# First layer: the gate's weights in one 48-column operand, norm vectors loaded by rows, the first head's projections ahead of the small tokens

## The chip, the core and the metric

The kernel runs on one core of a Trainium2 chip. The core has five engines that take their instructions in written order, each from its own queue: TensorE (PE, matrix products; its weight loads are listed apart as PEld), VectorE (DVE), ScalarE (ACT), GpSimd (POOL) and SyncE (SP), which here does nothing but issue DMA transfers. The metric is the device time of one execution in microseconds (us), as the median of several runs.

## The reference

One inference step of a two-layer decoder, in float32. There are 1024 prompt tokens, 16 "meta" tokens in front of them, and 8 sample tokens that continue running sequences, each of 1024 features. Layer one is gated linear attention (4 heads, keys of 128, values of 256), layer two differential attention with a paged cache; a squared-ReLU MLP of 4096 follows each. Cut to what matters here:

```python
def gla_project(x, w_in, w_gate, b_gate):
    h = x @ w_in
    q, k, v, r, g_low = jnp.split(h, [qk, 2 * qk, 2 * qk + vv, 2 * qk + 2 * vv], axis=-1)
    ...
    lg = jax.nn.log_sigmoid((g_low @ w_gate + b_gate).astype(F32)) / GLA_TAU

def gla_chunk(state, q, k, v, lg):
    b = jnp.cumsum(lg, axis=1)
    o_inter = jnp.einsum('blhd,bhde->blhe', q * jnp.exp(b), state)
    ...

def post_norm(x, f, g, b):
    return layer_norm(DEEPNORM_ALPHA * x + f, g, b)
```

`g_low` has 16 columns: the gate is a product with 16 columns of `w_in`, then one with the 16-row matrix `w_gate`.

## The kernel before

**Prompt tokens.** The 1024 prompt tokens are transposed by TensorE (L264) into XH and XL, the high and the low part of x, features on partitions, in two halves of 512 tokens (`c`). A product in near-float32 precision is three matmuls (`mm3`, L194 to L197): high by high, high by low, low by high. Weights come through `unit` (L171): four loads of 256 KB into `raw` (two buffers), a cast on ACT to `whi`, a subtraction on POOL to `wlo`. Two such units exist at a time. `qk_unit(h)` holds head h's q and k columns, `kunit(wi, 1024 + 256h)` its v columns.

**The gate.** `graw` holds the 16 gate columns; `ghi` and `glo` are its parts. For each half, eight blocks of features with three matmuls each go to a bank of PSUM, and a DVE copy brings 16 rows to `gT`: the first half of the tokens on partitions 0 to 15, the second on 32 to 47. `wg` holds `w_gate` twice, on the same partitions.

**Small tokens.** The 16 meta and 8 sample tokens stand together in `sx` (32 columns). They run through all of layer one, its MLP and the input projection of layer two in plain float32, with the small token block as the stationary operand in four column strips of 32 and the weights streaming through `swt` (two buffers of 1 MB). L280 and L285 are their input projection (eight and four loads of 1 MB), L413 their product with the eight running states, three buffers of which lie in Y (`stt`, loaded at L410, updated at L416). L449, L503 and L520 are the later matrices. `SM`, the state behind the meta tokens, is what the prompt's heads start from.

**Heads.** For each of four heads: q and k for both halves (96 matmuls of 512), v (192 matmuls of 256), then for each half the gate product L602, `log_gate` on ACT and DVE, a cumulative sum (L607), the products within 32-token blocks and at seven levels (L617, L632; elementwise work in `level`), and four steps that carry the state (L660 to L664). Products go to three banks named `mmt`, the rest of a head to three banks named `axt`, the small tokens to two named `smt`. Then the r projections with the output gate (L683 to L695), and the stage's pools close.

**Vectors.** `lnp` holds the four pairs of norm vectors with features on partitions: eight loads (L304), each gathering 1024 separate 4-byte elements. `bg` (L309, 512 elements) and `gn` (L564, 256) come in the same way.

**What sets the order.** The program is written in the order of the listing, but a planner orders each engine's instructions before the run: it walks a simulated time line and gives a free engine the ready instruction that was written first. The small tokens are written ahead of the heads, so the heads' projections fill the places where the small tokens wait. The hardware then keeps to that order, whatever really comes late. `tc.issue_after(ins)` places what is traced inside it behind `ins` on its queue.

Of the kernel before, what the change touches and what calls it, by code (L numbers as in the profile page):

```python
# [21 lines left out]
P = 128  # L22
D = 1024
T = 1024
NB = 8
# [3 lines left out]
GH = 4  # L29
# [81 lines left out]
def hybrid_step(ctx, tc, A, dbg=None, upto=9):  # L111
    nc = tc.nc
    V, S, G, TE = nc.vector, nc.scalar, nc.gpsimd, nc.tensor
    dma = nc.sync.dma_start
# [20 lines left out]
    def mmt():  # L135
        return banks["mm"].tile([P, 512], F32, name="mmt")

    def axt():
        return banks["ax"].tile([P, 512], F32, name="axt")

    def smt():
        return banks["sm"].tile([P, 512], F32, name="smt")

    def cload(name, pool=cp):
        a, b = CCOL[name]
        t = pool.tile([P, b - a], F32, name="c_" + name)
        dma(t, A["cf"][:, a:b])
        return t
# [8 lines left out]
    ident = cload("ident")  # L157
# [29 lines left out]
    def kunit(w, c0):  # L187
        return unit(256, w.rearrange("(k p) n -> p k n", p=P)[:, :, c0 : c0 + 256])

    def split(hi, lo, src, eng=V):  # L190
        S.copy(hi, src)
        return eng.tensor_tensor(lo, src, hi.bitcast(F32), op=ALU.subtract)  # L192

    def mm3(ps, ah, al, bh, bl, first, last):  # L194
        TE.matmul(ps, ah, bh, start=first, stop=False)  # L195
        TE.matmul(ps, ah, bl, start=False, stop=False)  # L196
        TE.matmul(ps, al, bh, start=False, stop=last)  # L197
# [3 lines left out]
    gp = p1.enter_context(tc.tile_pool(name="gp", bufs=1))  # L201
    g2 = p1.enter_context(tc.tile_pool(name="g2", bufs=2))
# [23 lines left out]
    def sload2(w, k, eng=None):  # L226

        t = swt()
        dma(t, w[k * P : (k + 2) * P, :].rearrange("(k p) n -> p k n", p=P))
        return t  # L230

    sx = gp.tile([P, NB, TS], F32, name="sx")
    masks = gp.tile([P, 5, TS], U8, name="masks")
    Ats = [gp.tile([P, 4, P], F32, name="At%d" % i) for i in range(2)]
# [12 lines left out]
    ps = smt()  # L247
# [3 lines left out]
    wi = A["gla_w_in"][0]  # L251
    wir = wi.rearrange("(k p) n -> p k n", p=P)

    def qk_unit(h):
        return unit(P, *[wir[:, :, 512 * i + h * P : 512 * i + (h + 1) * P] for i in range(2)])

    qku = qk_unit(0)
    for t in range(4, 8):
        dma(Yt[:, t, :], A["x_prompt"][0, t * P : (t + 1) * P, :])
    for c in range(2):  # L260
        for k in range(NB):
            ps = axt()
            for i in range(4):
                TE.transpose(ps[:, i * P : (i + 1) * P], Yt[:, 4 * c + i, k * P : (k + 1) * P], ident)  # L264
            cs = slice(512 * c, 512 * c + 512)
            split(XH[:, k, cs], XL[:, k, cs], ps)
# [1 line left out]
    mf = s4()[:, : 5 * TS]  # L268
    dma(mf, A["cm"].rearrange("p l t -> p (l t)"))
    V.tensor_copy(masks.rearrange("p l t -> p (l t)"), mf)  # L270
    graw = gp.tile([P, NB, 16], F32, name="graw")
    dma(graw, wir[:, :, 3072:3088])
    diag = cload("diag", gp)


    pa, pb = smt(), smt()
# [4 lines left out]
    for k in range(0, NB, 2):  # L281
        w = sload2(wi[:, 2048:3072], k)
        for i in range(2):
            for c in range(GH):
                TE.matmul(pb[c * TS : (c + 1) * TS, :256], sx[:, k + i, :], w[:, i, c * 256 : (c + 1) * 256], start=k + i == 0, stop=k + i == NB - 1)  # L285
    sqkv = s2()
    S.copy(sqkv, pa)
    sv = Y[:TS, 4096:5120]
# [9 lines left out]

    inv = cload("inv", gp)
    srope = cload("srope", gp)  # L300
    for i, nm in enumerate(("ln_mix", "ln_mlp")):
        for j, gb in enumerate("gb"):
            for l in range(2):
                dma(lnp[:, 2 * l + i, j, :], A[f"{nm}_{gb}"][l].rearrange("(k p) -> p k", p=P))  # L304
    wg = gp.tile([48, 512], F32, name="wg")
    for c in range(2):
        dma(wg[32 * c : 32 * c + 16, :], A["gla_w_gate"][0])
    bg = gp.tile([P, GH], F32, name="bg")
    dma(bg, A["gla_b_gate"][0].rearrange("(h p) -> p h", p=P))  # L309

    def log_gate(z, n, h):

        a = t2()[:, :n]
        S.activation(a, z, AF.Abs, bias=bg[:, h : h + 1])
        S.activation(a, a, AF.Exp, scale=-1.0)
        S.activation(a, a, AF.Ln, bias=1.0)
        m = t2()[:, :n]
        V.tensor_scalar(m, z, bg[:, h : h + 1], 0.0, ALU.add, ALU.min)
        V.tensor_tensor(m, m, a, op=ALU.subtract)
        return m  # L320

    ps = smt()
# [4 lines left out]
    ps = smt()  # L327
# [79 lines left out]
    for b in range(NS):  # L407
        stt = Y[:, 5120 + 1024 * (b % 3) : 6144 + 1024 * (b % 3)].rearrange("p (h e) -> p h e", e=256)
        vb = vbs[:, b % 2, :].rearrange("p (h e) -> p h e", e=256)
        dma(stt, A["state_gla"][0, b].rearrange("h d e -> d h e"))  # L410
        dma(vb.rearrange("p h e -> p (h e)"), A["vs"][b : b + 1, :].broadcast_to([P, D]))
        for h in range(GH):
            TE.matmul(po[h * TS : (h + 1) * TS, :256], qmk[:, h, b, :], stt[:, h, :], start=False, stop=b == NS - 1)  # L413
# [135 lines left out]
    dma(A["sxd"], sx)  # L549


    ghi = gp.tile([P, NB, 16], F32R, name="ghi")
    glo = gp.tile([P, NB, 16], F32R, name="glo")
# [9 lines left out]
    gn = gp.tile([P, 2], F32, name="gn")  # L563
    dma(gn, A["gla_norm"][0].rearrange("(m p) -> p m", p=P))  # L564
    gss = gp.tile([P, GH, 8], F32, name="gss")

    for h in range(GH):
        hi, lo = qku if h == 0 else qk_unit(h)
        hv, lv = (w.rearrange("p (i k n) -> p i k n", i=2, n=P) for w in (hi, lo))
        qk = {}  # L570
        for c in range(2):
            cs = slice(512 * c, 512 * c + 512)
            for i in range(2):
                ps = mmt()
                for k in range(NB):
                    mm3(ps, hv[:, i, k, :], lv[:, i, k, :], XH[:, k, cs], XL[:, k, cs], k == 0, k == NB - 1)
                t = g2.tile([P, 512], F32, name=("gq", "gk")[i])
                if i == 0:
                    S.activation(t, ps, AF.Copy, scale=P ** -0.5)
                else:  # L580
                    S.copy(t, ps)
                qk[c, i] = t
        hi, lo = kunit(wi, 1024 + h * 256)
        hv, lv = (w.rearrange("p (k n) -> p k n", n=256) for w in (hi, lo))
        vt = {}
        for c in range(2):
            v = Yh[:, h, 4 * c : 4 * c + 4, :]
            for i2 in range(2):
                ps = mmt()
                for i in range(2):  # L590
                    t = 4 * c + 2 * i2 + i
                    for k in range(NB):
                        a = slice(t * P, (t + 1) * P)
                        mm3(ps[:, i * 256 : (i + 1) * 256], XH[:, k, a], XL[:, k, a], hv[:, k, :], lv[:, k, :], k == 0, k == NB - 1)
                S.copy(v[:, 2 * i2 : 2 * i2 + 2, :].rearrange("p i e -> p (i e)"), ps)
            vt[c] = v
        st = SM[:, h, :]
        for c in range(2):
            q, k_, v = qk[c, 0], qk[c, 1], vt[c]
            cs = slice(512 * c, 512 * c + 512)  # L600
            ps = axt()
            TE.matmul(ps, wg[32 * c : 32 * c + 16, h * P : (h + 1) * P], gT[32 * c : 32 * c + 16, :], start=True, stop=True)  # L602
# [945 lines left out]
```

## Time and profile before

| | |
|---|---|
| median of 3 runs | 2934.85 us (2927.28, 2934.85, 2936.18) |
| profiled execution, its own time | 2915.81 us |
| its span, first to last instruction | 2914.1 us |
| mean granted TensorE clock | 0.978 |
| PE / PEld / DVE / ACT / POOL busy, share of the span | 96 / 78 / 64 / 36 / 39% |
| last output of the small tokens' chain issued | 410 us |
| first load of layer two issued | 506 us |

A line of the order of time reads: start in us, duration in us, engine, line of the kernel, operation, what is written and what is read, shape, number of instructions; in brackets, the idle time before it and who ended it. A line of waits reads: who waited, for whom, total us, times, longest. "SPq" is SyncE's queue of DMA issues. In a row by stretches, each engine has its busy time and its number of instructions in brackets; then come the granted clock (1.00 is full speed), the share of time in which the DMA engines were busy, and the rate. Durations of matmuls are modelled and overlap: the spacing of their starts is what they take.

### The profile page before, as it was taken

The page shows a single profiled execution, that of the slowest core. Times are in us where ns is not written, and L with a number is a line of the kernel's source. Part 1 is how long each engine was busy: PE and PEld are TensorE (multiplying, and loading weights), DVE is VectorE, ACT ScalarE, POOL GpSimd, SP SyncE. Part 2 cuts the span into 40 slices and gives each one's busy share as a digit, 9 for nine tenths or more (in the row PEclk, how much of TensorE's full clock was granted, in tenths as well). Part 3 has the DMA queues.
Part 4 walks back from the last instruction along what each step waited for, and adds up shares of the span by engine and source line. Part 5 has one row for each costly group of instructions (what it writes and reads, how often), then busy time and mean ns, then how long its engine had stood idle before and what let it go on. Part 6 is the DMA issues. An engine that isn't in the chain of part 4 may idle for free. (4 is left out here: it accounts for less than half of the span.)

```text
span 2914.1 us, 52192 instructions
## 1 busy us (share of the span) xinstructions
PE 2783.9 (96%) x19668; PEld 2275.1 (78%) x19668; DVE 1857.9 (64%) x2976; ACT 1038.3 (36%) x2071; POOL 1145.4 (39%) x885
## 2 busy tenths in 40 slices
PE   8999999999999999999989999989898999999996
PEld 5776668987777777777888986878788889797985
DVE  2664544458877877777676731878438755838378
ACT  2343354151122122122411111777325535345343
POOL 1321122234333333433323430122326766677666
PEclk9999999999999999999999998999899999999998
DMA  8667541524798888988488988463427878796972
GB/s 262 210 214 248 187 168 39 191 73 164 255 341 309 309 328 310 331 315 321 137 274 288 360 298 260 102 135 84 116 98 214 230 224 234 195 288 163 270 205 86
DMA packets 299308, 643.83 MB, mean 221 GB/s; under 512 B 35168, under 2 KB 150880, under 8 KB 287792
## 3 DMA queue, kind: packets, MB, share of 16 engines
q1 hardware_dynamic: 267520, 531.15, 52.8%
q0 software_dynamic: 31536, 109.35, 15.2%
q8 instruction: 155, 2.54, 0.3%
q14 instruction: 97, 0.79, 0.1%
HBM read 582.89 MB, written 40.91 MB: 214 GB/s over the span
## 5 line engine op out<-in xcount | busy, mean ns | idle before, releaser
L183 POOL TENSOR_TENSOR wlo<-raw,whi 128x512 fp32r<-128x512 f32 x256 | 361.2, 1425 | 786.0 <-ACT whi L182 697.6
L195 PE MATMUL mmt<-whi,XH 128*128 128x256 f32 (+1 forms) x1824 | 554.0, 305 | 7.5 <-DVE qr L1051 3.8
L196 PE MATMUL mmt<-wlo,XH 128*128 128x256 f32 (+1 forms) x1824 | 550.8, 303 | 0.5 <-POOL wlo L183 0.5
L195 PE MATMUL mmt<-XH,whi 128*128 128x512 f32 (+1 forms) x1376 | 480.1, 350 | 15.7 <-DVE HL L192 6.4
L197 PE MATMUL mmt<-XH,wlo 128*128 128x512 f32 (+1 forms) x1376 | 479.4, 350 | 0.0
L197 PE MATMUL mmt<-whi,XL 128*128 128x256 f32 x1536 | 440.5, 287 | 6.8 <-DVE XL L192 6.8
L195 PEld LDWEIGHTS mmt<-whi,XH 128*128 128x128 f32 x1824 | 346.3, 190 | 43.6 <-issue 19.8
L182 ACT CAST whi<-raw 128x512 fp32r<-128x512 f32 x256 | 152.4, 619 | 619.0 <-PE mmt L197 247.3
L196 PEld LDWEIGHTS mmt<-wlo,XH 128*128 128x128 f32 x1824 | 346.6, 190 | 25.0 <-issue 11.7
L771 DVE TENSOR_REDUCE sc<-pg 128x16 f32<-128x1024 f32 x256 | 309.6, 1214 | 78.4 <-POOL pg L770 74.9
L197 PEld LDWEIGHTS mmt<-whi,XL 128*128 128x128 f32 x1536 | 292.3, 190 | 22.7 <-issue 14.8
L196 PE MATMUL mmt<-XL,whi 128*128 128x512 f32 x768 | 307.6, 400 | 0.0
L195 PEld LDWEIGHTS mmt<-XH,whi 128*128 128x128 f32 x1376 | 261.2, 190 | 57.5 <-DVE HL L192 8.2
L770 DVE TENSOR_TENSOR pg<-pg,qb 128x1024 f32<-128x1024 f32 x192 | 261.3, 1366 | 59.1 <-DMA pg<-in_cache_k 42.9
L197 PEld LDWEIGHTS mmt<-XH,wlo 128*128 128x128 f32 x1376 | 261.2, 190 | 43.6 <-issue 12.0
L770 POOL TENSOR_TENSOR pg<-pg,qb 128x1024 f32<-128x1024 f32 x64 | 156.3, 2443 | 286.3 <-DMA pg<-in_cache_k 215.0
L195 PE MATMUL mmt<-whi,HH 128*128 128x512 f32 x512 | 205.3, 401 | 1.4 <-DVE Y L995 1.4
L196 PE MATMUL mmt<-wlo,HH 128*128 128x512 f32 x512 | 204.5, 399 | 0.0
L197 PE MATMUL mmt<-whi,HL 128*128 128x512 f32 x512 | 203.7, 398 | 0.0
L196 PEld LDWEIGHTS mmt<-XL,whi 128*128 128x128 f32 x768 | 145.2, 189 | 40.4 <-issue 8.9
L196 PE MATMUL mmt<-XH,whi 128*128 128x258 f32 x608 | 173.0, 286 | 3.7 <-DMA XH<-xc 2.9
L1397 POOL TENSOR_TENSOR wlo<-RW,whi 128x512 fp32r<-128x512 f32 x96 | 152.4, 1678 | 56.6 <-ACT whi L1396 56.5
(432 smaller groups left out, 5482.1 us busy)
## 6 DMA issues: line engine op xcount, KB each, us to landing
pg<-in_cache_k SPq DMA_DIRECT2D x256, 512.0 KB
pg<-in_cache_v SPq DMA_DIRECT2D x256, 512.0 KB
XH<-xc POOLq DMA_DIRECT2D x42, 1032.0 KB, 8.8
raw<-in_mlp_w SPq DMA_DIRECT2D x164, 256.0 KB
rw<-in_mlp_w SPq DMA_DIRECT2D x156, 256.0 KB
swt<-in_mlp_w SPq DMA_DIRECT2D x32, 1024.0 KB
RW<-in_mlp_w POOLq DMA_DIRECT2D x96, 256.0 KB, 7.3
xc<-XH POOLq DMA_DIRECT2D x14, 1032.0 KB, 8.0
```

Source lines behind the costliest of these rows:

```text
L182: S.copy(hi[:, c], raw)
L183: G.tensor_tensor(lo[:, c], raw, hi[:, c].bitcast(F32), op=ALU.subtract)
L195: TE.matmul(ps, ah, bh, start=first, stop=False)
L196: TE.matmul(ps, ah, bl, start=False, stop=False)
L197: TE.matmul(ps, al, bh, start=False, stop=last)
L770: eng.tensor_tensor(pg, pg, qb, op=ALU.mult)
L771: return V.tensor_reduce(sc[:, n, :], pg.rearrange("p (h d) -> p h d", d=64), op=ALU.add, axis=AX.X).ins
L1397: G.tensor_tensor(lo[:, k, :], t, hi[:, k, :].bitcast(F32), op=ALU.subtract)
```

## The change

The stage of layer one is changed in these ways; nothing of layer two is.

1. The gate's high and low parts stand in one 48-column operand `gw` (high in columns 0 to 15, zeros, low in 32 to 47). Each block of features is multiplied with XH and with XL, 2 matmuls in place of 3, and two groups of 16 rows of the result are added. The product of low part and low part is thereby included.
2. The norm vectors, the gate's bias and the output norm are loaded by six transfers of rows of 128 elements into one tile, turned by one transpose, and spread by four copies.
3. `proj(h)` holds a head's q, k and v projections. The gate and `proj(0)` are written ahead of the small tokens' input projection; the first head's v weights are loaded ahead of the transposes.
4. The states' loads are placed behind the last load of the small tokens' input weights on SyncE's queue.
5. For each head both halves' gate products are written one behind the other, each with a bank of its own, ahead of the work of the halves.

```diff
@@ sload2
-        dma(t, w[k * P : (k + 2) * P, :].rearrange("(k p) n -> p k n", p=P))
+        swl.append(dma(t, w[k * P : (k + 2) * P, :].rearrange("(k p) n -> p k n", p=P)).ins)
...
@@ before the transposes of x
+    v0u = kunit(wi, 1024)
+    graw = gp.tile([P, NB, 16], F32, name="graw")
+    dma(graw, wir[:, :, 3072:3088])
...
@@ behind the load of the masks
-    graw = gp.tile([P, NB, 16], F32, name="graw")
-    dma(graw, wir[:, :, 3072:3088])
     diag = cload("diag", gp)
+
+    prow = s2()[:, :P]
+    for i, nm in enumerate(("ln_mix", "ln_mlp")):
+        for j, gb in enumerate("gb"):
+            dma(prow[32 * i + 16 * j : 32 * i + 16 * j + 16, :], A[f"{nm}_{gb}"].rearrange("l (k p) -> (l k) p", p=P))
+    dma(prow[64:68, :], A["gla_b_gate"].rearrange("l (h p) -> (l h) p", p=P))
+    dma(prow[68:70, :], A["gla_norm"].rearrange("l (m p) -> (l m) p", p=P))
+    ps = smt()
+    TE.transpose(ps[:, :70], prow[:70, :], ident[:70, :70])
+    for i in range(2):
+        V.tensor_copy(lnp[:, i::2].rearrange("p l j k -> p j l k"), ps[:, 32 * i : 32 * i + 32].rearrange("p (j l k) -> p j l k", j=2, l=2))
+    bg = gp.tile([P, GH], F32, name="bg")
+    V.tensor_copy(bg, ps[:, 64:68])
+    gn = gp.tile([P, 2], F32, name="gn")
+    V.tensor_copy(gn, ps[:, 68:70])
+
+    def proj(h):
+        hi, lo = qku if h == 0 else qk_unit(h)
...
+                for k in range(NB):
+                    mm3(ps, hv[:, i, k, :], lv[:, i, k, :], XH[:, k, cs], XL[:, k, cs], k == 0, k == NB - 1)
...
+        hi, lo = v0u if h == 0 else kunit(wi, 1024 + h * 256)
...
+        return qk
+
+    gw = gp.tile([P, NB, 48], F32R, name="gw")
+    gz = s4()[:, : NB * 48].rearrange("p (k n) -> p k n", n=48)
+    V.memset(gz, 0.0)
+    V.tensor_copy(gz[:, :, :16], graw)
+    S.copy(gw, gz)
+    V.tensor_tensor(gw[:, :, 32:], graw, gw[:, :, :16].bitcast(F32), op=ALU.subtract)
+    gT = gp.tile([48, 512], F32, name="gT")
+    for c in range(2):
+        ps = mmt()
+        for k in range(NB):
+            for i, x in enumerate((XH, XL)):
+                TE.matmul(ps[:48, :], gw[:, k, :], x[:, k, 512 * c : 512 * c + 512], start=k + i == 0, stop=k + i == NB)
+        ga, gb_, go = ps[32 * c : 32 * c + 16, :], ps[32 - 32 * c : 48 - 32 * c, :], gT[32 * c : 32 * c + 16, :]
+        S.copy(go, gb_)
+        V.tensor_tensor(go, go, ga, op=ALU.add)
+    first = proj(0)
...
@@ behind the small tokens' input projection
+    w_in = swl[-1]
...
-    for i, nm in enumerate(("ln_mix", "ln_mlp")):
-        for j, gb in enumerate("gb"):
-            for l in range(2):
-                dma(lnp[:, 2 * l + i, j, :], A[f"{nm}_{gb}"][l].rearrange("(k p) -> p k", p=P))
...
-    dma(bg, A["gla_b_gate"][0].rearrange("(h p) -> p h", p=P))
...
@@ the loop over the states
-        dma(stt, A["state_gla"][0, b].rearrange("h d e -> d h e"))
+        with tc.issue_after(w_in):
+            dma(stt, A["state_gla"][0, b].rearrange("h d e -> d h e"))
...
@@ behind the small tokens
-    split(ghi, glo, graw)
-    gT = gp.tile([48, 512], F32, name="gT")
-    for c in range(2):
-        cs = slice(512 * c, 512 * c + 512)
-        ps = mmt()
-        for k in range(NB):
-            mm3(ps[:16, :], ghi[:, k, :], glo[:, k, :], XH[:, k, cs], XL[:, k, cs], k == 0, k == NB - 1)
-        V.tensor_copy(gT[32 * c : 32 * c + 16, :], ps[:16, :])
...
     for h in range(GH):
-        hi, lo = qku if h == 0 else qk_unit(h)
...
+        qk = first if h == 0 else proj(h)
+        st = SM[:, h, :]
+        pgs = [axt() for c in range(2)]
         for c in range(2):
+            TE.matmul(pgs[c], wg[32 * c : 32 * c + 16, h * P : (h + 1) * P], gT[32 * c : 32 * c + 16, :], start=True, stop=True)
+        for c in range(2):
+            q, k_, v = qk[c, 0], qk[c, 1], Yh[:, h, 4 * c : 4 * c + 4, :]
...
-            ps = axt()
-            TE.matmul(ps, wg[32 * c : 32 * c + 16, h * P : (h + 1) * P], gT[32 * c : 32 * c + 16, :], start=True, stop=True)
-            m = log_gate(ps, 512, h)
+            m = log_gate(pgs[c], 512, h)
```

More of the change, by code (lines that the diff above doesn't have):

```diff
@@ L228, in sload2 @@
         t = swt()
-        dma(t, w[k * P : (k + 2) * P, :].rearrange("(k p) n -> p k n", p=P))
+        swl.append(dma(t, w[k * P : (k + 2) * P, :].rearrange("(k p) n -> p k n", p=P)).ins)
         return t
+    swl = []
     sx = gp.tile([P, NB, TS], F32, name="sx")
@@ new lines, in hybrid_step @@
+    ps = smt()
[8 more added lines that the diff above has]
+        hi, lo = qku if h == 0 else qk_unit(h)
+        hv, lv = (w.rearrange("p (i k n) -> p i k n", i=2, n=P) for w in (hi, lo))
+        qk = {}
+        for c in range(2):
+            cs = slice(512 * c, 512 * c + 512)
+            for i in range(2):
+                ps = mmt()
+                for k in range(NB):
+                    mm3(ps, hv[:, i, k, :], lv[:, i, k, :], XH[:, k, cs], XL[:, k, cs], k == 0, k == NB - 1)
+                t = g2.tile([P, 512], F32, name=("gq", "gk")[i])
+                if i == 0:
+                    S.activation(t, ps, AF.Copy, scale=P ** -0.5)
+                else:
+                    S.copy(t, ps)
+                qk[c, i] = t
+        hi, lo = v0u if h == 0 else kunit(wi, 1024 + h * 256)
+        hv, lv = (w.rearrange("p (k n) -> p k n", n=256) for w in (hi, lo))
+        for c in range(2):
+            for i2 in range(2):
+                ps = mmt()
+                for i in range(2):
+                    t = 4 * c + 2 * i2 + i
+                    for k in range(NB):
+                        a = slice(t * P, (t + 1) * P)
+                        mm3(ps[:, i * 256 : (i + 1) * 256], XH[:, k, a], XL[:, k, a], hv[:, k, :], lv[:, k, :], k == 0, k == NB - 1)
+                S.copy(Yh[:, h, 4 * c + 2 * i2 : 4 * c + 2 * i2 + 2, :].rearrange("p i e -> p (i e)"), ps)
+        return qk
@@ new lines, in hybrid_step @@
+    gw = gp.tile([P, NB, 48], F32R, name="gw")
[5 more added lines that the diff above has]
+    gT = gp.tile([48, 512], F32, name="gT")
+    for c in range(2):
+        ps = mmt()
+        for k in range(NB):
+            for i, x in enumerate((XH, XL)):
[3 more added lines that the diff above has]
+        V.tensor_tensor(go, go, ga, op=ALU.add)
@@ L307, in hybrid_step @@
         dma(wg[32 * c : 32 * c + 16, :], A["gla_w_gate"][0])
-    bg = gp.tile([P, GH], F32, name="bg")
-    dma(bg, A["gla_b_gate"][0].rearrange("(h p) -> p h", p=P))
     def log_gate(z, n, h):
@@ L549, in hybrid_step @@
     dma(A["sxd"], sx)
-    ghi = gp.tile([P, NB, 16], F32R, name="ghi")
-    glo = gp.tile([P, NB, 16], F32R, name="glo")
-    split(ghi, glo, graw)
-    gT = gp.tile([48, 512], F32, name="gT")
-    for c in range(2):
-        cs = slice(512 * c, 512 * c + 512)
-        ps = mmt()
-        for k in range(NB):
-            mm3(ps[:16, :], ghi[:, k, :], glo[:, k, :], XH[:, k, cs], XL[:, k, cs], k == 0, k == NB - 1)
-        V.tensor_copy(gT[32 * c : 32 * c + 16, :], ps[:16, :])
-    gn = gp.tile([P, 2], F32, name="gn")
@@ L564, in hybrid_step @@
-    dma(gn, A["gla_norm"][0].rearrange("(m p) -> p m", p=P))
     gss = gp.tile([P, GH, 8], F32, name="gss")
     for h in range(GH):
-        hi, lo = qku if h == 0 else qk_unit(h)
-        hv, lv = (w.rearrange("p (i k n) -> p i k n", i=2, n=P) for w in (hi, lo))
-        qk = {}
+        qk = first if h == 0 else proj(h)
+        st = SM[:, h, :]
+        pgs = [axt() for c in range(2)]
         for c in range(2):
+            TE.matmul(pgs[c], wg[32 * c : 32 * c + 16, h * P : (h + 1) * P], gT[32 * c : 32 * c + 16, :], start=True, stop=True)
@@ L572, in hybrid_step @@
+        for c in range(2):
+            q, k_, v = qk[c, 0], qk[c, 1], Yh[:, h, 4 * c : 4 * c + 4, :]
             cs = slice(512 * c, 512 * c + 512)
[L573 to L600, printed above, removed]
-            ps = axt()
-            TE.matmul(ps, wg[32 * c : 32 * c + 16, h * P : (h + 1) * P], gT[32 * c : 32 * c + 16, :], start=True, stop=True)
-            m = log_gate(ps, 512, h)
+            m = log_gate(pgs[c], 512, h)
             b = g2.tile([P, 512], F32, name="gb")
```

## The prediction

> **What bounds the kernel now.** I read the page first, then the stretches of the first layer, then TensorE's waits there. The page:
>
> ```profile
> span 2914.1 us, 52192 instructions
> PE 2783.9 (96%) x19668; PEld 2275.1 (78%) x19668; DVE 1857.9 (64%) x2976; ACT 1038.3 (36%) x2071; POOL 1145.4 (39%) x885
> ```
>
> TensorE is busy 96% of the span, so what takes work from it, or idle time out of its queue, counts; relief for another engine does not by itself. The stretches (start:end, length, then busy time and instructions of PE, PEld, DVE, ACT, POOL, then clock, DMA share, GB/s):
>
> ```profile
> 0.00:50.00 50.00, 36.90 (x184) 21.33 (x185) 15.77 (x29) 14.79 (x26) 8.95 (x11) 0.97 0.92 279
> 50.00:100.00 50.00, 50.00 (x385) 38.56 (x384) 11.30 (x41) 14.19 (x39) 10.49 (x8) 1.00 0.65 222
> 100.00:150.00 50.00, 45.97 (x489) 35.13 (x489) 38.00 (x74) 15.86 (x38) 20.41 (x12) 0.93 0.67 205
> ...
> 20.00:510.00 490.00, 467.25 (x4438) 344.23 (x4437) 240.70 (x526) 191.11 (x458) 112.30 (x70) 0.99 0.56 184
> ```
>
> The stage that the change touches lasts to about 510 us. Behind the first 20 us, TensorE idles there for 490 - 467.25 = 22.75 us, and its clock dips in two of the stretches shown. Who ended those waits (from 0 to 700 us; microseconds in total, times, longest):
>
> ```profile
> PE axt L264 <- DMA Y<-in_x_prompt: 6.7, 4, 5.4
> PE smt L280 <- DMA swt<-in_gla_w_in: 4.1, 1, 4.1
> PE smt L413 <- DMA Y<-in_state_gla: 3.9, 3, 2.1
> PE mmt L195 <- ACT Y L595: 2.8, 2, 2.3
> ...
> PE axt L617 <- DVE t L357: 2.4, 3, 1.4
> ```
>
> The first is the opening load of x and stays. The second and third are the ones within reach. TensorE's order of time around the second:
>
> ```profile
> 34.50 0.39 PE L195 MATMUL mmt<-XH,ghi 128*16 128x512 f32 x1
> 38.98 1.19 PE L280 MATMUL smt<-swt,sx 128*32 128x512 f32 x8 [4.09 <-DMA swt<-in_gla_w_in]
> 40.10 0.61 PE L196 MATMUL mmt<-XL,ghi 128*16 128x512 f32 x1
> ...
> 43.37 0.40 PE L195 MATMUL mmt<-XH,ghi 128*16 128x512 f32 x1
> 43.60 0.39 PE L196 MATMUL mmt<-XL,ghi 128*16 128x512 f32 x1
> ```
>
> TensorE takes its instructions in written order: it stands 4.09 us before the third block of the small tokens' input weights, while the gate's matmuls behind it have all they need. Eight matmuls then start from 40.10 to 43.37, 0.41 us apart instead of 0.23 (43.37 to 43.60): 3.27 - 8 x 0.23 = 1.4 us more, for the lowered clock. Why the block is late is in SyncE's queue and in the DMA rate:
>
> ```profile
> 19.76 0.43 SPq L304 DMA_DIRECT2D lnp<-in_ln_mix_g  x1
> 20.24 2.47 SPq L304 DMA_DIRECT2D lnp<-in_ln_mix_b  x1
> ...
> 29.25 1.08 SPq L307 DMA_DIRECT2D wg<-in_gla_w_gate  x2
> ...
> 31.96 0.38 SPq L223 DMA_DIRECT2D swt<-in_gla_w_in  x1
> ...
> 34.16 5.57 SPq L410 DMA_DIRECT2D Y<-in_state_gla  x3
> ```
> ```profile
> 22.00:34.00 12.00, 12.00 (x70) 6.25 (x69) 3.68 (x6) 3.39 (x6) 2.54 (x2) 1.00 0.73 71
> ...
> 70.00:86.00 16.00, 16.00 (x171) 12.78 (x169) 3.71 (x21) 6.78 (x20) 5.08 (x4) 1.00 0.91 302
> ```
>
> Seven of the eight loads of the norm vectors, each 4-byte elements strewn over partitions, hold SyncE from 19.76 to 29.25. In that time the DMA engines are 73% busy and move 71 GB/s, where 91% moves 302 later. The weight block is issued only at 31.96, with three loads of states behind it that share the engines.
>
> **The change part by part.**
>
> *The gate's weights.* Before, 48 matmuls of 512 moving columns, in three groups of 16 (two of them below):
>
> ```profile
> L195 PE MATMUL mmt<-XH,ghi x16: 388/398/628, 19.5 to 45.8; 128*16 128x512 f32 x16
> ...
> L197 PE MATMUL mmt<-XH,glo x16: 388/396/628, 26.3 to 46.3; 128*16 128x512 f32 x16
> ```
>
> After, high and low part stand in one 48-column operand and 32 matmuls do the work. Spacing is 0.23 us at 16 columns, so 16 fewer give **-3.7 us**. The head projections, with 128 columns, have the same spacing, so 48 columns are not dearer:
>
> ```profile
> 46.99 0.39 PE L195 MATMUL mmt<-XH,whi 128*128 128x512 f32 x1
> 47.22 0.40 PE L196 MATMUL mmt<-XL,whi 128*128 128x512 f32 x1
> ```
>
> The operand needs a memset, two copies and a subtraction on DVE and ACT, which in 0 to 100 us are under a third busy; the sum of the two parts is a copy on ACT and an add on DVE in place of one DVE copy. Its scratch follows the mask load in a one-buffer pool; if that load is late the projection of q for the first 512 tokens (24 x 0.23 = 5.5 us) covers it. Uncovered it would cost those few us. I take 0.
>
> *Norm vectors by rows.* Ten strewn loads (eight of lnp, bg, gn) become six of 512-byte rows, one transpose and four small DVE copies. The transpose costs TensorE at most what four cost, 0.60 us:
>
> ```profile
> 29.69 0.60 PE L264 MATMUL axt<-c_ident,Y 128*128 128x128 f32 x4
> ```
>
> I take **+0.2**. The DMA time is off the path except through the stall above.
>
> *First head first; states after the input weights.* The 4.09 us and the slow clock go with the late block: nothing the first head needs waits for it, its weights are asked for before it, and the states stand behind it. **-5.5 us** (bounds -5.5 and 0, if another late load takes the place). Moved with it are 288 matmuls of q, k, v: 96 x 0.23 + 192 x 0.12 = 45 us by
>
> ```profile
> 74.99 0.28 PE L195 MATMUL mmt<-whi,XH 128*128 128x256 f32 x1
> 75.11 0.28 PE L196 MATMUL mmt<-wlo,XH 128*128 128x256 f32 x1
> ```
>
> They used to fill the gaps between the small tokens' blocks. Now those blocks come behind them: with 20 us of opening, 3.7 of transposes, 7.4 of gate and 45 of projections, the hand-over is near 75 us. Two staging buffers exist, so 10 of these 12 loads wait for it:
>
> ```profile
> swt<-in_gla_w_in SPq DMA_DIRECT2D x12, 1024.0 KB
> ```
>
> At 302 GB/s, 10.5 MB take 35 us. What TensorE has meanwhile:
>
> ```profile
> 25.28 1.06 PE L280 MATMUL smt<-swt,sx 128*32 128x512 f32 x8
> ...
> 84.96 1.07 PE L285 MATMUL smt<-swt,sx 128*32 128x256 f32 x16
> ...
> 104.52 1.12 PE L602 MATMUL axt<-gT,wg 16*128 16x512 f32 x2
> 105.57 0.44 PE L617 MATMUL axt<-gq,gk 128*32 128x32 f32 x26
> ```
>
> The blocks themselves, 6 x 1.06 + 4 x 1.07 = 10.6 us; the next head's q and k as far as three PSUM banks go, 72 x 0.23 = 16.6; the first head's own gate and levels, some 5 (an estimate from the rows above: 1.05 for a gate, about 0.5 for each of seven sets of small products and the diagonal). Together 32 against 35. I take **+1** here (bounds 0 and +20, below). The small tokens' chain runs some 20 us later; it has room:
>
> ```profile
> 410.13 0.32 SPq L546 DMA_DIRECT2D out_v_rows_s<-s  x1
> ```
>
> Its last output is issued at 410, 100 us ahead of the stage's end, and TensorE's remaining work is what ends that stage. So the delay itself is 0.
>
> *Both gate products of a head together.* Each takes 1.05 us (104.52 to 105.57), eight in all. They read partitions 0 to 15 and 32 to 47 and write two banks. No row shows two row strips at work at once. The nearest, L280 above, has four column strips share 1.06 us, about what L602 takes alone. By that row a pair costs one: 4 x 1.05 = -4.2; without overlap 0; and a bank held through the half could cost about what the small products (L617) already wait for DVE, 2.4. I take the middle between -4.2 and 0, **-2.1**. The Trainium skill, TensorEngine Tiling (Array Packing), section Tiling Modes, says that tiles on different rows can load and multiply in parallel; by it the sum would hold the whole -4.2, which no run so far shows for rows.
>
> *The states' loop* keeps its three buffers. Its 3.9 us could go or, with the first three loads no longer early, grow by about as much. I take 0 (bounds -7 with the clock it loses, and +4).
>
> Sum: -3.7 + 0.2 - 5.5 + 1 - 2.1 = **-10.1 us**. The profiled execution took 2915.81 us for its span of 2914.1, so 2905.7 for such a one. The runs shown have the median 2934.85 (2927.28 to 2936.18), 19 above it; subtracted there: **2924.7 us**. Layer two's buffers open when this stage's close, so it starts earlier by the same amount.
>
> **The rivals.**
>
> *Slower: a hole at the hand-over.* For it: 32 us of work against 35 of loads leaves nothing over, and SyncE's queue has stood still before, from 86.09 to 107.10:
>
> ```profile
> 86.09 0.38 SPq L229 DMA_DIRECT2D swt<-in_gla_w_out  x1
> 107.10 1.61 SPq L180 DMA_DIRECT2D raw<-in_gla_w_in  x2
> ```
>
> If it stands so on the next head's weights, their 16.6 us of projections are missing where they are needed, and the loads of the small tokens behind them stop too. With the clock:
>
> ```profile
> 120.00:130.00 10.00, 8.13 (x160) 5.69 (x158) 10.00 (x23) 3.48 (x11) 2.20 (x1) 0.83 0.75 218
> 130.00:140.00 10.00, 7.92 (x95) 6.03 (x94) 8.52 (x19) 2.46 (x6) 4.95 (x2) 0.83 0.85 265
> ```
>
> 20 us at 0.83 lose 3.4, so +20 in all, and -11.1 + 20 = +9: 2943.8. It decides from a hole of 11 us. Against it: the first head frees its weight buffers from about 53 us, long before. The Trainium skill, TensorE: Matmul & The Clock Gate, Part 1, puts the lower clock only behind an idle window of some 3.4 us; by that a hole in short pieces would cost 16.6 and no more. The trace differs: in these two stretches no wait was over 2.1 us, and the clock fell.
>
> *Hidden.* The stall is replaced by one of its size at the hand-over and row strips do not overlap, so the edit of the pair does not do what it says: -3.7 + 0.2 = -3.5, 2931.4. For it: 18 us of other waits in the stage that just move about.
>
> *More.* The pair overlaps wholly, the hand-over is free, and the states' waits go with their clock: -3.7 + 0.2 - 5.5 - 4.2 - 6.6 = -20: 2915. For it: the first head's elementwise work starts near 80 instead of 105, so DVE is less crowded where the states are updated. Against it: the loop is three buffers deep either way.
>
> **How the numbers follow.** Forecast 0.42, more 0.15, hidden 0.26, slower 0.17. About 0.3%, 8.8 us, can be told from no change here, so 2926.0 and 2943.7 part the cases. Of the forecast's own range (-6 to -15, 2920 to 2929) four fifths lie below: 0.34 + 0.15 = 0.49 faster; 0.08 + 0.26 = 0.34 the same; 0.17 slower. The range takes in more, the forecast and hidden, and cuts into the slower: 2912 to 2940.
>
> **What would show it.** Of the changed kernel: no wait of L280 on its weights before 70 us and records of 0.4 us from 20 us on; over 200 GB/s between 22 and 34 us; 32 gate matmuls; the two gate products of a head starting within 0.2 us and done in about 1.1 (or 2.1, if rows do not overlap); PE busy near 35 of the 35 us behind the hand-over. A gap of over 11 us there, or small tokens that end past the last head, would make the prediction wrong.

## The result, and the profile after

The change makes the kernel **slower, by 0.6%**: median 2947.22 us against 2927.41 for the kernel before, 20 runs of each on the same chips, a ratio of 1.0064 with a 95% interval of [1.0052, 1.0076]. That is +19.8 us, where -10.1 was forecast. (The kernel before is a few us quicker here than in the three runs shown ahead of the prediction; the medians below are always set against runs of it on the same chip, and "us over" or "under" is the difference of these two medians.)

The head of the page of the changed kernel:

```profile
span 2948.4 us, 52160 instructions
PE 2790.8 (95%) x19653; PEld 2285.0 (77%) x19653; DVE 1854.8 (63%) x2982; ACT 1040.4 (35%) x2074; POOL 1139.2 (39%) x885
```

Thirty-two instructions fewer, and TensorE is still busy 7 us longer. Both numbers hide what happened, so the first layer has to be cut into stretches. (One trace is one execution: the two spans differ by 34.3 us, and 11.7 us of that lie behind the first load of layer two, where the program is not changed. In the traces of this study that part lasts from 2406 to 2428 us, so a stage is read from its trace, and what a version is worth from the medians.) First the kernel before, to the first load of layer two (columns as ahead of the prediction: PE, PEld, DVE, ACT, POOL, clock, DMA share, GB/s):

```profile
20.00:100.00 80.00, 75.91 (x514) 51.75 (x513) 17.77 (x53) 20.43 (x50) 16.74 (x12) 0.98 0.75 231
100.00:200.00 100.00, 95.29 (x1041) 74.03 (x1040) 72.90 (x163) 41.13 (x108) 28.20 (x18) 0.97 0.62 200
200.00:400.00 200.00, 189.04 (x2156) 133.24 (x2155) 103.15 (x220) 73.56 (x195) 43.38 (x24) 1.00 0.66 230
400.00:506.00 106.00, 103.01 (x698) 81.21 (x697) 45.26 (x87) 53.48 (x105) 22.08 (x16) 1.00 0.15 49
```

and the changed kernel:

```profile
20.00:100.00 80.00, 78.61 (x490) 60.80 (x491) 7.84 (x18) 17.10 (x30) 17.91 (x14) 1.00 0.46 149
100.00:200.00 100.00, 71.66 (x859) 49.56 (x858) 64.95 (x158) 34.85 (x99) 23.60 (x13) 0.73 0.71 239
200.00:400.00 200.00, 192.32 (x2045) 140.60 (x2033) 103.55 (x227) 76.05 (x202) 36.22 (x23) 0.99 0.63 220
400.00:528.00 128.00, 123.89 (x1020) 96.25 (x1013) 61.99 (x122) 62.51 (x128) 32.42 (x19) 0.99 0.27 87
```

The stretch from 20 to 100 us got better, as forecast: fuller, at full clock. The one from 100 to 200 fell apart: 28 us idle in place of 5, and the clock 0.73 in place of 0.97. From 20 us to the stage's end TensorE idles 508 - 466.48 = 41.5 us (before 486 - 463.25 = 22.75), and the time it is busy below full speed, busy time times (1 - clock), loses 22.4 us (before 4.4); summed over stretches of 10 us it is 20.3 (before 4.4). So idle time +18.8, clock +16 to +18. The busy time at full speed is 13 to 15 us smaller; 3.7 of this are the gate's matmuls and 3.2 three pairs of gate products (below), the rest I can't assign, since the durations of overlapping matmuls are modelled. The sum is +22 us, which is what SyncE's queue shows: the first load of layer two goes out at 528.85 instead of 506.24.

Where TensorE waited up to 220 us (for whom; total, times, longest):

```profile
PE smt L474 <- DMA Y<-in_state_gla: 6.4, 3, 4.0
PE mmt L195 <- ACT Y L319: 6.0, 1, 6.0
...
PE smt L350 <- DMA swt<-in_gla_w_in: 4.9, 3, 3.2
```

The line numbers have moved: L345 and L350 are the small tokens' input products (before L280, L285), L334 the gate, L474 the product with the states (L413), L620, L638 and L653 a head's gate and small products (L602, L617, L632). No single wait is large. The stall that the prediction took away is gone from this list. The stretch by tens of microseconds:

```profile
90.00:100.00 10.00, 10.00 (x51) 6.76 (x44) 0.00 (x0) 0.00 (x0) 1.41 (x2) 1.00 0.78 259
100.00:110.00 10.00, 6.57 (x59) 3.09 (x57) 0.18 (x1) 1.74 (x3) 0.00 (x0) 0.90 0.87 310
110.00:120.00 10.00, 8.29 (x61) 4.00 (x60) 3.95 (x22) 3.52 (x15) 0.00 (x0) 0.50 0.93 322
120.00:130.00 10.00, 7.13 (x54) 5.12 (x56) 7.51 (x26) 4.31 (x13) 4.28 (x2) 0.50 0.65 246
130.00:140.00 10.00, 5.60 (x96) 2.89 (x88) 9.97 (x25) 4.26 (x14) 0.00 (x0) 0.50 0.32 91
140.00:150.00 10.00, 2.96 (x114) 2.09 (x112) 8.65 (x18) 3.85 (x8) 4.80 (x2) 0.50 0.81 259
...
103.00:150.90 47.90, 28.45 (x360) 16.14 (x352) 30.92 (x91) 17.68 (x53) 9.28 (x4) 0.55 0.73 247
```

From 90 to 100 us TensorE is full while DVE and ACT stand still; behind 110 they are the ones at work, and TensorE thins out at half clock. The last row is the time without any projection, from the end of the next head's first ones to the one that follows at 150.94: 19.45 us idle, and about 28.45 x 0.45 = 12.8 us lost to the clock, together 32 us in one hole. TensorE's own order of time there:

```profile
79.61 1.13 PE L620 MATMUL axt<-gT,wg 16*128 16x512 f32 x4
80.67 0.46 PE L638 MATMUL axt<-gq,gk 128*32 128x32 f32 x32
...
102.70 1.06 PE L345 MATMUL smt<-swt,sx 128*32 128x512 f32 x8
106.93 1.07 PE L350 MATMUL smt<-swt,sx 128*32 128x256 f32 x16 [3.16 <-DMA swt<-in_gla_w_in]
...
117.40 1.94 PE L350 MATMUL smt<-swt,sx 128*32 128x256 f32 x16 [1.44 <-DMA swt<-in_gla_w_in]
136.39 1.49 PE L653 MATMUL axt<-t 128*32 128x64 f32 x32 [2.87 <-DVE t L417]
...
144.71 1.08 PE L474 MATMUL smt<-Y,s 128*32 128x256 f32 x8 [3.97 <-DMA Y<-in_state_gla]
```

The first head's gate is multiplied from 79.61 to 80.7. ScalarE takes the result 46 us later. DVE, which had been without work for 46.47 us, copies the first head's diagonal at 81.20, at once, and then has nothing more to do until 108.70:

```profile
126.78 0.69 ACT L374 ACTIVATE t<-axt,bg 128x512 f32<-128x512 f32 x1
...
147.87 0.60 ACT L305 ACTIVATE gq<-mmt 128x512 f32<-128x512 f32 x1 [2.49 <-DVE t L417]
```
```profile
81.20 0.29 DVE L641 TENSOR_TENSOR gAd<-axt,c_diag 128x128 f32<-128x128 f32 x1 [46.47 <-PE axt L638]
```

The row at 147.87 is the next head's q leaving its `mmt` bank. Until then its q and k hold all three banks, for `gq` and `gk` are still in use by the first head's levels (L417), and these start only behind 126.78. So TensorE has more projections to do, but no bank to write them to.

SyncE's issues, and what held them:

```profile
78.88 1.20 SPq L223 DMA_DIRECT2D swt<-in_gla_w_in  x2
...
112.73 1.93 SPq L471 DMA_DIRECT2D Y<-in_state_gla  x3
...
435.48 0.33 SPq L607 DMA_DIRECT2D out_v_rows_s<-s  x1
...
528.85 0.35 SPq L740 DMA_DIRECT2D ptab<-in_page_table  x1
```
```profile
SPq L223 <- PE smt L345: 25.2, 5, 15.2
```

SyncE waits 15.2 us for TensorE to give back one of the two weight buffers, because TensorE stands in the first head's projections; nine of the twelve weight blocks go out from 78.88 to 112.7, the states behind them.

### The profile page after: what moved, and what is told of

It reads as the page before. It is cut to its first block, busy times and chain, and to the rows that moved or that the text cites. A ratio compares the mean times of both kernels' runs of the same rounds, so it can differ in the third digit from the quotient of the medians.

```text
span 2948.4 us, 52160 instructions
## 1 busy us (share of the span) xinstructions
PE 2790.8 (95%) x19653; PEld 2285.0 (77%) x19653; DVE 1854.8 (63%) x2982; ACT 1040.4 (35%) x2074; POOL 1139.2 (39%) x885
## 3 DMA queue, kind: packets, MB, share of 16 engines
q0 software_dynamic: 31536, 109.35, 15.2%
```

## The experiments

The expectations weigh these accounts. Cover (A): the projections put ahead are missing as the work that used to fill the small tokens' waits. Buffers (C): the first head's elementwise work waits, because the `t2` buffers that `log_gate` needs go to the small tokens first; its rival (D) says that those buffers cost little. End of the stage (S): the r outputs lie in `swt`, which the small tokens hold until their end, and they now end later.

**The order alone, and everything but the order.** The first kernel is the one before with `proj(0)`, the gate in its 48 matmuls and the early loads ahead of the small tokens. The second is the changed kernel with the head's projections back in the loop; the gate and the early loads stay ahead in it:

```diff
@@ the changed kernel
-    first = proj(0)
...
-        qk = first if h == 0 else proj(h)
+        qk = proj(h)
```

> The kernel before with one part of the change: gate (still 48 matmuls) and first head's projections written ahead of the small tokens, its v weights and the gate's columns loaded early. Norm vectors by elements, states unordered, gate products apart, all as before. Theory A (lost cover: the projections no longer fill the small tokens' waits): slower than before by 15 to 30 us, PE idle over 20 us between 100 and 200 us of the span. Rival B (the loss comes from the states put behind the input weights, from the pair holding a bank, or from the loads by rows): within 6 us of before, PE idle there under 10 us.

> The changed kernel with the first head's projections written back in the loop over the heads, behind the small tokens; all else of the change stays (gate in 48 columns and ahead, rows, states behind the input weights, pairs). Theory A: faster than before by 6 to 14 us (gate 3.7, stall 5.5, pairs 3.2, less what moves about), PE idle between 100 and 200 us near the 5 us of before. Rival B: still slower than before by 10 us or more.

Order alone: 2964.72 us, 1.0123 [1.0094, 1.0152], 36 us over the kernel before. All but the order: **2910.79 us, 0.9933 [0.9907, 0.9959], 18 us under it**. 36 - 18 = 18, and both together measured 19.8: the order costs some 36 us on the kernel before (there the gate moves with the projections) and 38 on the rest of the change, and this rest is worth 18. The second is the fastest kernel of this study and beats both. From 100 to 200 us, the order alone

```profile
100.00:200.00 100.00, 73.16 (x830) 47.10 (x822) 61.94 (x152) 32.15 (x96) 23.00 (x13) 0.71 0.71 234
```

has the hole of the changed kernel, and without the order

```profile
100.00:200.00 100.00, 91.75 (x963) 71.82 (x962) 73.59 (x160) 38.63 (x105) 35.84 (x19) 0.95 0.58 183
...
497.55 0.36 SPq L739 DMA_DIRECT2D ptab<-in_page_table  x1
```

it is nearly closed, and layer two begins 9 us sooner than before in its trace.

**Is that work filler?** If the projections are cover, then leaving some out gains where they stand ahead, and nothing where they fill. In the first head, 128 of the 192 v matmuls are left out (15.0 us of TensorE), in the changed kernel and in the one with late projections:

```diff
+                        if h == 0:
+                            TE.matmul(ps[:, i * 256 : (i + 1) * 256], XH[:, k, a], hv[:, k, :], start=k == 0, stop=k == NB - 1)
+                            continue
```

> The changed kernel with work left out: of the first head's v, only the product of the high parts is computed (64 of 192 matmuls, 128 x 0.117 = 15.0 us of TensorE less). Theory A (moved ahead, the projections stand on the small tokens' path): the hand-over comes 15 us earlier and the time falls by 9 to 16 us. Rival (TensorE's sum of work is what counts, whatever the order): the same 12 to 15 here and in the run with the projections behind.

> The same work left out of the kernel with the projections behind the small tokens. Theory A (there the projections fill waits of the small tokens): taking 15 us of filler away gives less than 8 us, and PE idle between 60 and 200 us grows by about what is not gained. Rival (sum of work): 12 to 15 us faster than that kernel.

Ahead of the small tokens the cut gains: 2938.62 us, 1.0033 [1.0016, 1.0051], 9.4 over the kernel before where the whole change is 19.8 over. The two weight buffers are given back 14 us sooner (the next two blocks go out at 64.63, not 78.88), and the stretch from 100 to 200 us stays as empty as it was, 28.1 us idle. In the loop it gains nothing: 2913.57 us, 0.9955 [0.9937, 0.9973], 15.7 under, where 18 under was measured without the cut. The missing work turns up as idle time there, 19.8 us in the stretch where it was 8.25:

```profile
100.00:200.00 100.00, 80.17 (x911) 62.43 (x910) 74.47 (x155) 36.20 (x99) 29.87 (x17) 0.85 0.57 180
```

The same 128 matmuls are worth ten microseconds in one place and nothing in the other. This is the clearest evidence for cover.

**Half as much ahead.** Only q and k of the first head ahead, v in the loop:

```diff
+        return qk
+
+    def projv(h):
...
         qk = first if h == 0 else proj(h)
+        projv(h)
```

> The changed kernel, but only the first head's q and k (96 matmuls, 22 us) stay ahead of the small tokens; its v (192 matmuls, 22.5 us) goes back into the loop over the heads. Theory A (each matmul moved ahead is missing as cover for the small tokens' waits): about half of the dose, PE idle between 100 and 200 us under 14 us and the time 15 to 32 us under the changed kernel's, that is 15 us under to 5 us over before. Rival (the input weights come late because anything big is ahead of them): still 10 us or more over before.

2937.03 us, 1.0027 [1.0012, 1.0043], 7.7 over: better than the whole order, by 12, where 15 to 32 were expected; the rival's ten or more over isn't met either. Half of the 45 us moved back gives a third of the loss back, and the stretch from 100 to 200 stays three quarters full at a clock of 0.84:

```profile
100.00:200.00 100.00, 75.41 (x857) 57.87 (x856) 70.06 (x158) 33.17 (x92) 24.46 (x15) 0.84 0.57 189
```

**The first head's buffers.** The small tokens get two small buffers of their own:

```diff
+    spool2 = p1.enter_context(tc.tile_pool(name="spool2", bufs=2))
...
-        a = t2()[:, :n]
+        a = (u2() if n == TS else t2())[:, :n]
...
-        u = t2()[:, :128]
+        u = u2()
```

> The changed kernel, projections still first, but the small tokens no longer share the five elementwise buffers (t2) of the heads: two small buffers of their own, and the turned keys of the meta tokens in the scratch of the states' queries. Theory C (the hole is there because the first head's elementwise work gets its buffers only behind the small tokens' chain: its gate products end at 80.7 us and ScalarE takes them up at 126.8): ScalarE takes them up before 90 us, PE idle between 100 and 200 us falls from 28 to under 14 us, and the time is 12 to 28 us under the changed kernel's, near or below before. Rival D (the hole is the wait for weights and states as such, which own buffers do not shorten): the first head starts early but the time stays within 8 us of the changed kernel's.

> Both: projections behind the small tokens again, and own buffers for the small tokens. Theory A and C: faster than before by 8 to 18 us; the own buffers let the first head start earlier than 104 us, yet its projections last until about 100 anyway, so at most 4 us better than projections behind alone. Rival: own buffers are worth 5 us or more here too, since the heads' elementwise work is then free of the small tokens through the whole stage.

On the changed kernel: 2939.94 us, 1.0036 [1.0015, 1.0057], 11 over. C is right on the start: ScalarE takes the gate a microsecond after the product,

```profile
81.68 0.69 ACT L378 ACTIVATE t<-axt,bg 128x512 f32<-128x512 f32 x1 [1.28 <-PE axt L624]
...
100.00:200.00 100.00, 88.56 (x912) 69.77 (x912) 60.62 (x136) 32.65 (x90) 26.56 (x17) 0.96 0.60 199
200.00:400.00 200.00, 184.43 (x2142) 131.25 (x2143) 113.22 (x260) 80.53 (x213) 38.30 (x23) 0.95 0.63 221
400.00:518.00 118.00, 110.22 (x765) 81.46 (x764) 42.95 (x86) 43.72 (x96) 22.39 (x16) 0.99 0.36 122
```

and the hole between 100 and 200 closes to 11.4 us. It is wrong on the size: some 9 us are gained, where C forecast 12 to 28 and D at most 8, for idle time and low clock come back from 200 us on (15.6 us idle at 0.95, and 7.8 behind 400, where the changed kernel had 7.7 at 0.99, and 4.1). Work done earlier is work missing later. With late projections the buffers bring nothing: 2917.28 us, 0.9957 [0.9938, 0.9976], 11.5 under where 18 under was had without them. With own buffers on both sides the order costs 11.1 + 11.5 = 22.6 us, without them 38. So the queueing for `t2` is real and sets where the hole stands, and up to 15 us of the loss may be its work; more than half of the loss is there without it.

**The end of the stage.** The r outputs in another pool, on the changed kernel, on the one with own buffers and on the one with late projections:

```diff
-        silt = swt().rearrange("p k (c n) -> p k c n", c=2)
         for c in range(2):
+            silt = s4().rearrange("p (k n) -> p k n", n=512)
```

> The changed kernel with the r projections' outputs in the scratch that the small tokens' hidden values leave free, not in the small tokens' two weight buffers. Theory S (the late chain of the small tokens holds the r projections, and so carries the loss to the stage's end): 8 us or more under the changed kernel, below 2939, and the first such output comes before the chain's end. Rival (the idle time is lost where it stands, between 100 and 200 us): within 5 us of the changed kernel.

> The changed kernel with own elementwise buffers for the small tokens (as before under that name: 2939.9) and the r outputs out of the weight buffers. Theory S: the idle time that own buffers only moved to 400 to 500 us is filled; 8 us or more under the run with own buffers, so below 2932. Rival: within 5 us of it.

> The kernel with the projections behind the small tokens (2910.8) and the r outputs out of the weight buffers. Theory S would let r work fill the small tokens' last waits: up to 5 us under that kernel. Rival: one buffer in place of two halves for the r outputs makes them wait for the update that reads them, 3 us or more over.

2953.27 us, 1.0091 [1.0068, 1.0115], 26 over, so 6 worse than the change; 2937.32, 1.0043 [1.0026, 1.0061], the same as own buffers alone; 2926.33, 0.9996 [0.9977, 1.0016], 17 worse than late projections alone. S falls: in the first of these the r outputs do begin 22 us ahead of the small tokens' last output, and 20 us sooner than in the changed kernel (429.57),

```profile
409.06 0.60 ACT L709 ACTIVATE s<-mmt 128x512 f32<-128x512 f32 x1
...
431.44 0.33 SPq L607 DMA_DIRECT2D out_v_rows_s<-s  x1
```

and nothing is won by it. In the third, the 12 us by which its trace has layer two start later stand behind 400 us: there TensorE idles 8.5 us at a clock of 0.94, where late projections alone have 1.15 at 1.00. That fits the rival of its expectation, one buffer that makes the r outputs wait, in place and sign.

**The parts that were worth 18.** Each alone on the kernel before. Norm vectors by rows (the diff of part 2 of the change, and nothing else), both gate products of a head together (part 5), and the states behind the input weights (part 4):

```diff
@@ the pair
+        pgs = [axt() for c in range(2)]
+        for c in range(2):
+            TE.matmul(pgs[c], wg[32 * c : 32 * c + 16, h * P : (h + 1) * P], gT[32 * c : 32 * c + 16, :], start=True, stop=True)
...
@@ the states
+        with tc.issue_after(w_in):
+            dma(stt, A["state_gla"][0, b].rearrange("h d e -> d h e"))
```

> The kernel before with the norm vectors, the gate's bias and the output norm loaded by rows; nothing else. If the strewn loads cause the stall at 35 to 39 us: it goes, 3 to 8 us faster. If the states' loads cause it: the wait for the third weight block stays over 2 us and the time is within 3 us of before.

> The kernel before with both gate products of a head written together; nothing else. Row strips work at once in the changed kernel's trace (two products in 1.06 us), so up to 4 x 1.05 = 4.2 us faster; if the bank that is held costs as much, within 3 us of before; slower by 3 us or more if it costs more.

> The kernel before with the states' loads placed behind the last load of the small tokens' input weights; nothing else. If the three states (1.5 MB) behind the third weight block are what makes the block late: the wait of 4.1 us goes and the time is 3 to 10 us lower. If the strewn loads are: the wait stays, within 3 us of before.

Rows: 2919.43 us, 0.9962 [0.9945, 0.9979], **10 under**, and no wait of TensorE at all from 20 to 100 us:

```profile
20.00:100.00 80.00, 80.00 (x596) 55.74 (x594) 18.39 (x54) 21.92 (x53) 16.98 (x13) 1.00 0.72 246
...
22.00:34.00 12.00, 12.00 (x66) 6.18 (x65) 3.71 (x6) 5.24 (x9) 3.80 (x3) 1.00 0.94 304
```

The pair: 2931.64, 1.0004 [0.9987, 1.0021]. The states: 2927.29, 0.9993 [0.9976, 1.001], and the stall on the third block stays, 3.6 us:

```profile
PE smt L281 <- DMA swt<-in_gla_w_in: 3.6, 1, 3.6
```

So it was the strewn loads that made the block late, not the states behind it. That the end of the stall pays for the 10 us is not shown: in the traced execution of this kernel (2927.20 us) the first load of layer two goes out at 513.48, 7 us later than before, with 16.2 us idle from 200 to 400 us, where before had 11.

The gate in 48 columns, once in its old place behind the small tokens, once written ahead of them:

```diff
-        for k in range(NB):
-            mm3(ps[:16, :], ghi[:, k, :], glo[:, k, :], XH[:, k, cs], XL[:, k, cs], k == 0, k == NB - 1)
+    gz = s4()[:, : NB * 48].rearrange("p (k n) -> p k n", n=48)
...
+            for i, x in enumerate((XH, XL)):
+                TE.matmul(ps[:48, :], gw[:, k, :], x[:, k, 512 * c : 512 * c + 512], start=k + i == 0, stop=k + i == NB)
```

> The kernel before with the gate's weights in 48 columns, in their old place; nothing else. By the sum of the prediction: 3.7 us faster (32 matmuls at 0.23 us). Rival: the scratch follows other uses of its one buffer (the queries of the states, the hidden tokens), which delays the gate behind the small tokens and makes it slower by 5 us or more.

> The kernel before with the gate in 48 columns, written ahead of the small tokens, its scratch therefore free early; the projections stay behind. By the prediction's term: 3.7 us faster; with the gate's matmuls gone as filler before the late weight block the wait there may grow, so 0 to 6 faster. Rival: the gate ahead pushes the small tokens back like the projections do, slower by 3 us or more.

In the old place: 3114.56 us, 1.0624 [1.0601, 1.0647], **185 over**. The scratch `gz` comes from a pool of one buffer, which the small tokens use again and again, so the gate's matmuls start only at 270.21, and no head can go past its projections until then:

```profile
100.00:200.00 100.00, 40.77 (x186) 7.60 (x190) 20.37 (x47) 1.53 (x5) 11.93 (x7) 0.50 0.77 261
...
696.76 0.35 SPq L723 DMA_DIRECT2D ptab<-in_page_table  x1
```

The run thereby shows the small tokens' chain with no heads to fill it: TensorE at 41%, at half clock. Written ahead: 2939.46, 1.0042 [1.0028, 1.0056], 10 over. TensorE waits there for the operand, which ScalarE copies late. ScalarE first waits 3.26 us for a load of head weights that was issued among the strewn loads, and the copy comes behind the cast of these weights on its queue:

```profile
PE mmt L286 <- DVE gw L280: 5.1, 1, 5.1
...
27.51 0.62 ACT L182 CAST whi<-raw 128x512 fp32r<-128x512 f32 x1 [3.26 <-DMA raw<-in_gla_w_in]
28.03 0.51 ACT L279 CAST gw<-s 128x384 fp32r<-128x384 f32 x1
...
20.00:60.00 40.00, 34.90 (x171) 19.89 (x173) 8.09 (x14) 9.20 (x16) 7.65 (x6) 0.91 0.91 263
```

This wait takes the place of the stall of 4.1 us, so it is not the whole 10. From 100 to 200 us there are 10.7 us idle at a clock of 0.93, where before had 4.7 at 0.97, and 7.5 behind 400, where before had 3; why, no run here shows. The rival (the gate pushes the small tokens back) has the sign, but their third block starts at 39.61, 0.6 us later than before.

The last takes one part away from the late projections, the placing of the states:

```diff
-        with tc.issue_after(w_in):
-            dma(stt, A["state_gla"][0, b].rearrange("h d e -> d h e"))
+        dma(stt, A["state_gla"][0, b].rearrange("h d e -> d h e"))
```

> The changed kernel with the projections behind the small tokens (as in the run of that name) and the states' loads free again, not behind the input weights. If placing the states is what makes that kernel better than the sum of its parts: 4 us or more slower than it (2910.8), that is 8 to 14 us faster than before. If the planner places them late anyway once the strewn loads are gone: within 4 us of it.

2928.64 us, 0.9995 [0.9981, 1.0009]: the whole 18 is gone, though the same part alone brings 0. In the traces, layer two starts 6.5 us later than with it (504.02 and 497.55); the rest of the 17 is not to be seen in this stage. The parts don't add: -10 for rows, +10 for the gate ahead, 0 and 0 make 0, not -18. Own buffers, the r outputs' pool and the states each take 6 to 17 us from the best version. What these edits may have in common is that the planner lays out the stage anew after each, and that each layout meets the chain's waits otherwise; no run here tests that. **Which part pays for the 18 stays open.**

## Why the prediction was wrong

**The step that failed** is the one of the hand-over: "I take +1 here (bounds 0 and +20, below)", with the sentence behind it, "So the delay itself is 0". It measured **+36 to +38**. It compared TensorE's work with the *loads* behind the hand-over, 32 us against 35, and that comparison was nearly right: from 78.9 to 112.7 us the blocks go out, TensorE is fully busy from 90 to 100, waits 3.16 and 1.44 us for two blocks, and has the last at 119. What it left out is the work behind the loads. The small tokens' chain goes on in short steps on DVE and ACT (the levels to about 130 us, the states' loop to about 180), and before the change the first heads' projections lay between these steps. Moved ahead, 45 us of them were done by 78, the next head's q and k were done as far as three banks go by 103, and then no other projection could go out until 150.94, because the first head's elementwise work, which frees the banks, came behind the small tokens'. With own buffers it doesn't, that hole closes, and the order still costs 22.6 us. I had used the right sentence of the front matter, that the projections fill the places where the small tokens wait, for the input weights only.

"It has room" was right in itself: the chain's last output is issued at 435.48, 93 us ahead of the stage's end. But room at its end doesn't make a delay free. A chain that has to be covered costs what its cover lacks, wherever it ends. The 128 matmuls left out in either place show this. Most of the signs that the prediction named came true (full clock, 281 GB/s, 32 gate matmuls, TensorE busy 31.3 of the 35 us behind the hand-over at 77.75, no gap of 11 us in them). Only one of them, the end of the small tokens' chain, looked past 113 us.

**The clock doubled it.** Bounds of +20 held 3.4 us for the clock; the stage lost 16 to 18 us more to it than before, about as much as to idle time. For 40 us the clock is 0.50, though no wait of TensorE was longer than 4 us.

**The rival "slower"** named the place and the sign, and it got a chance of 0.17. Its cause was another: SyncE did stand still, 15.2 us, but for a buffer of the small tokens' weights, not for the next head's, and TensorE was busy meanwhile. The hole came later, and was worth +20 in all, where the rival had +9.

**The gate's weights, -3.7:** right as matmul time. The 32 matmuls run 0.23 us apart from 25.11 to 32.4 us, so 48 columns cost no more than 16:

```profile
25.11 0.48 PE L334 MATMUL mmt<-XH,gw 128*48 128x512 f32 x1
...
32.40 0.39 PE L334 MATMUL mmt<-XL,gw 128*48 128x512 f32 x1
```

"Uncovered it would cost those few us" came true as a wait, 5.1 us, in the run with the gate written ahead, though for a late weight load on ScalarE's queue and not for the masks; the time there was +10, more than the wait.

**Rows and the stall, -5.5 + 0.2:** right on the stall, which goes. In time the rows alone measured -10 (interval -16 to -6), but their trace doesn't show it as the stall's price. In the changed kernel, from 22 to 34 us,

```profile
22.00:34.00 12.00, 11.36 (x59) 6.58 (x59) 4.90 (x8) 6.18 (x11) 3.90 (x4) 1.00 0.83 281
```

the rate is 281 GB/s where it was 71, the clock full. That the states had to move for this was wrong; moved alone they change nothing.

**The pair, -2.1:** the mechanism is there. Four records, both halves' products, take 1.06 us from 79.61 to the next start (two passes per half: before, one half took as long). In three of the four heads they ran together, in one apart: 3 x 1.05 = 3.2 us of TensorE. The rule of the Trainium skill, TensorEngine Tiling (Array Packing), section Tiling Modes, that tiles on different rows can load and multiply in parallel, agrees with these rows. In the time of the kernel it can't be told from nothing.

**The states' loop, 0:** its waits grew from 3.9 to 6.4 us, inside the bounds of -7 and +4.

Without the moved projections the remaining terms of the sum, -11.1, would have forecast the right sign for the version that measured -18. As the parts don't add, this agreement is in part luck.

## What to carry to other kernels

Work that waits for nothing is the filler of everything that does. Before it is moved ahead, list every wait that it fills, to the end of the chain it covers and not just to the next load, and ask what fills them afterwards, and which buffers and banks that needs. Price the clock beside the gap: here it cost about as much again. And where a planner lays out a stage, take an edit of a few microseconds for proven only when it holds in more than one company: here one part was worth 0 alone and 17 beside the others.

## What was not expected of the hardware

- **The clock stays down without a long wait.** From 110 to 130 us TensorE is shown 83% and 71% busy, at a clock of 0.50 throughout. It comes back once projections run without a break: they start 0.43 us apart at 150.94, and 0.23 apart from 155.8, after some 4.7 us. The Trainium skill, TensorE: Matmul & The Clock Gate, Part 1, has half rate as the throttled state, an idle window of about 3.4 us as what brings it, and a busy window of that length as what releases it. The 0.50 agrees with it, and the return, 4.7 us, took no less than that. The same part also tells of a clock that swings when TensorE idles often and briefly; the prediction read it too narrowly when it took a hole in short pieces to cost no clock. Why 83% busy in short pieces was not enough, no run here shows.
- **Two row strips at once.** Products of 16 rows on partitions 0 to 15 and 32 to 47 take 1.06 us together, about what one takes alone (1.05).
- **Strewn loads cost more than their bytes.** While loads of 1024 separate elements of 4 bytes went out (seven of the eight), the DMA engines were 73% busy at 71 GB/s; by rows, in the same 12 us, they moved 304 GB/s at 94%, and the kernel was 10 us faster.
